# Modulation weights between the units of a projection pair, the tokens' norm ahead of the memory's projections, GpSimd for the first low parts, gates behind the picks' rows

## The chip, the cores and the metric

The kernel runs on one core of a Trainium2 chip. The metric is the device time of one execution, in microseconds (us). TensorE multiplies matrices, VectorE (DVE in rows) and ScalarE (ACT) do elementwise work, GpSimd (POOL) does elementwise work and issues gathers, and SyncE (SP) issues the loads from HBM (the device's main memory).

## The reference

All is float32; there are 256 tokens of width 1024. Three parts follow each other, cut here to what matters:

```python
# block 1: one layer
h = rms_norm(x, g_mix); proj = h @ w_in            # 1024 -> 4352: three attentions' q, k, v
y_sb, y_dil, y_mem = stick_breaking(...), dilated(...), memory_attention(m_q, rms_norm(mem, g_mem))
gates = sigmoid(h @ w_gate + b_gate)
x = x + (gates[:,:,0]*y_sb + gates[:,:,1]*y_dil + gates[:,:,2]*y_mem) @ w_out
# product-key experts ("peer"): 8 heads, 16 picks of 16384 each
h2 = rms_norm(x, g_ffn); q = (h2 @ w_q).reshape(T, 8, 2, 128)
s1, i1 = top_k(sc[:, :, 0], 16); s2, i2 = top_k(sc[:, :, 1], 16)   # two lists of 128 scores
cand = s1[..., :, None] + s2[..., None, :]; top_s, pos = top_k(cand, 16)
idx = take_along(i1 * 128 + i2, pos); gate = softmax(top_s)
x = x + sum_k gate_k * gelu(u[idx_k] . h2) * v[idx_k]
# two diffusion-style layers: an mLSTM and a retention mixer, each followed by 16 experts (MoE);
# six modulation vectors per layer come from a condition vector: silu(c) @ ada_w + ada_b
```

The modulation vectors depend on the condition alone. Their weights (`ada_w`) can be loaded and multiplied at any time before the mixers.

## The kernel before, in words

Weights stream from HBM in slabs of 1 MB (128 partitions by 2048 floats) through a ring of slots, four of them in block 1. SyncE issues every load in the order in which the program asks for the slabs, and a load waits until its slot is free. A weight slab is two *units*. Each unit is split into a rounded high part on ScalarE (L608) and a low part, source minus high, on VectorE or GpSimd (L615); a list, `units.lo`, says which of the two engines makes the next low part (`None` is VectorE). The parts go to tiles named `rw_68` to `rw_71`, so at most four units are split at a time, at most two of them ahead of the unit in use. Three matrix products per tile (`mm3`, all at L627) then make up for a product in float32. The activations' two parts lie in `rt` tiles.

*Block 1* (`block1`): the memory's norm, its projection to keys and values in two pairs of slabs (`wide`, two slabs or four units, 48 matmuls of 512 columns), then the tokens' projections (`proj_task`), into which the three attentions are woven as side tasks. Twelve of the projections are pairs (`pair` 6 times, the gates 6 times). The modulation vectors are a task of their own, `ada_task`: one step of it takes one `ada_w` slab out of the ring and multiplies it (8 matmuls of 32 rows by 256 columns, 16 records in the trace), and a projection says how many steps follow it. A modulation slab is not split; its slot is free when its 8 matmuls are done.

*Peer* (`prepare`, `route`, `picks`): `prepare` makes scores in eight slabs of queries; after slabs 0, 1, 3 and 7 it runs `route` for the heads at hand, which finds the 16 best picks of each head on VectorE: top-16 of two lists (MAX8, FIND_INDEX8, MATCH_REPLACE8), of their sums, the softmax over the 16 (`gate`), and the row numbers (`rows`), whose last operation is the cast at L1481. `picks` then gathers, for each pick, a row of 8 KB for each of 128 tokens (256 gathers by GpSimd, L1352), multiplies it with the tokens on VectorE, and needs `gate` only after a Gelu over a batch of picks. The rest of `prepare` and the mLSTM's context are woven into the gathers.

The two mixers and the two MoE layers follow (`block2`); the MoE layers only stream weights and multiply them. A scheduler sets the final order on each engine from the program's order and its dependencies, so that an edit can also move instructions far from it.

Of the kernel before, what the change touches and what calls it, by code (L numbers as in the profile page):

```python
# [14 lines left out]
AF = mybir.ActivationFunctionType  # L15
OP = mybir.AluOpType
AX = mybir.AxisListType
# [492 lines left out]
class K:  # L510
# [264 lines left out]
                         (w[u][0].a[:, s], w[u][1].a[:, s]), c == 0, c == nk - 1)  # L775
        return p

    def wide(self, Ts, units):


        ps = [[self.ps() for _ in range(2)] for _ in Ts]
        for k, unit in enumerate(units):
            w = self.units.get(*unit)
            for T, p in zip(Ts, ps):
                for i in range(2):
                    for cc in range(2):
                        c = 2 * k + cc
                        h, f = slice(c * 256 + i * 128, c * 256 + i * 128 + 128), slice(cc * 512, (cc + 1) * 512)
                        self.mm3(p[i].a, (T[0].a[:, h], T[1].a[:, h]), (w[0].a[:, f], w[1].a[:, f]), c == 0, c == 2 * len(units) - 1)
            for b in w:  # L790
                b.free()
        return ps

    def halves(self, kind, s, *x):
# [51 lines left out]
    def block1(self, mem):  # L846
        mT = self.norm_T([m.a for m in mem], self.col("g_mem"), w=1024)
        for m in mem:
            m.free()
        self.ada_open()  # L850
        self.ada = self.ada_task([(0, k) for k in range(6)] + [(1, 0), (1, 1)])
        self.mkv = self.f(2048)

        mkv = self.mkv.v("p (i f) -> p i f", i=2)
        for s in range(2):
            for i, p in enumerate(self.wide([mT], self.halves("w1", 2 * s))[0]):
                self.act(mkv[:, i, s * 512:(s + 1) * 512], p.a)
                p.free()
            if s == 0:
                self.hT = self.norm_T([x.a for x in self.x], self.col("g_mix"))  # L860
        for b in mT:
            b.free()
        self.dil_buffers()
        self.drive(self.proj_task(), [self.mem_task(), self.sb_task(), self.dil_task()], 0.6)
        self.merge_task()
# [12 lines left out]
    def proj_task(self):  # L878
        nc = self.nc
        sbq = self.sbq.v("p (h t) -> p h t", h=8)  # L880
        nc.gpsimd.memset(self.sbq.a, 0.0)
        hT, W = self.hT, W1

        def pair(name, s, place):

            for i, p in enumerate(self.wide([hT], self.halves("w1", W[name] + 2 * s))[0]):
                for dst, a, b in place(i):
                    self.act(dst, p.a[:, a:b])
                p.free()
            self.ada_steps(2)  # L890

        def row(b, i, n, o=0):
            return b.a[:, i * n + o:i * n + o + 512]

        self.mq = self.f(2 * 512)
        pair("mq", 0, lambda i: [(row(self.mq, i, 512), 0, 512)])
        self.done.add("mq")
        yield 9800
        for s in range(4):
            w = self.wslab(("w1", W["sbqk"] + s))  # L900
            p = self.slab_T(hT, w)
            if s < 2:
                pv = p.v("p (b t) -> p b t", b=2)
                o = sbq[:, 4 * s:4 * s + 4].rearrange("p (b e) t -> p b e t", e=2)
                self.act(o[:64, :, 0], pv[:64])
                self.act(o[64:, :, 1], pv[64:])
            else:
                self.act(self.sbk.a[:, (s - 2) * 512:(s - 1) * 512], p.a)
            p.free()
            self.wfree(w)  # L910
            self.ada_steps(1)
            yield 5200
        pair("sbv", 0, lambda i: [(row(self.sbv, i, 512), 0, 512)])
        self.done.add("sbv")
        yield 9800
        for s in range(4):

            parts = []
            while len(self.dqkv) < (512 * s + 511) // 768 + 1:
                self.dqkv.append(self.f(2 * 768))  # L920
            for x in range(3):
                a, b = max(512 * s, 768 * x), min(512 * (s + 1), 768 * (x + 1))
                if a < b:
                    parts.append((x, a, b))
            pair("d", s, lambda i: [(self.dqkv[x].a[:, i * 768 + a - 768 * x:i * 768 + b - 768 * x], a - 512 * s, b - 512 * s) for x, a, b in parts])
            yield 9800
        w = self.wslab(("w1", W["dlast"]))
        p = self.slab_row(hT, w)
        self.act(self.dqkv[2].v("p (i f) -> p i f", i=2)[:, :, 512:], p.v("p (i f) -> p i f", i=2))
        p.free()  # L930
        self.wfree(w)
        self.done.add("dlast")
        self.ada_steps(1)
        yield 5200
        for s in range(6):
            if s % 2 == 0:
                self.gates.append(self.f(2048))
            b = self.bcast_row(f"bg{s // 2}", s % 2 * 512, 512)
            for i, p in enumerate(self.wide([hT], self.halves("w1", W["gate"] + 2 * s))[0]):
                o = row(self.gates[-1], i, 1024, s % 2 * 512)  # L940
                self.tt(o, p.a, b.a, OP.add)
                p.free()
            b.free()
            self.ada_steps(2)
            yield 9800

    def sb_task(self):
# [348 lines left out]
    def prepare(self, h2T):  # L1296

        self.sc = [self.plain(self.RA) for _ in range(2)]
        sub = self.stream.get(("w1", W1["sub"]))
        for s in range(8):  # L1300
            w = self.wslab(("w1", W1["pq"] + s))
            p = self.slab_T(h2T, w)
            q = self.f(512)
            self.act(q.a, p.a)
            p.free()
            self.wfree(w)
            p = self.ps()
            for i in range(2):
                for f in range(2):
                    self.mm(p.a[:, i * 256 + f * 128:i * 256 + f * 128 + 128], q.a[:, f * 256 + i * 128:f * 256 + i * 128 + 128],  # L1310
                            sub.a[:, (2 * s + f) * 128:(2 * s + f + 1) * 128])
            for i in range(2):
                self.act(self.sc[i].a[:, s * 256:(s + 1) * 256], p.a[:, i * 256:(i + 1) * 256])
            p.free(), q.free()
            yield 5200
            if s == 7:
                for b in h2T:
                    b.free()
                sub.free()
                self.stream.shrink(2)  # L1320
                self.units.lo = deque([None])
            if s in (0, 1, 3, 7):
                yield from self.route(0, {0: 0, 1: 1, 3: 2, 7: 4}[s], s + 1)
# [68 lines left out]
    def route(self, i, h0, h1):  # L1392

        V, n = self.nc.vector, h1 - h0
# [25 lines left out]
        top, pos = self.f(16 * n), self.f(16 * n)  # L1420
        tv = top.v("p (h k) -> p h k", h=n)
# [12 lines left out]
        gate, k1, k2 = r["gate"].a[:, c16], self.f(16 * n), self.f(16 * n)  # L1434
        pf = self.f(16 * n)
        V.tensor_copy(pf.a, pos.a.bitcast(U32))

        gv = gate.rearrange("p (h k) -> p h k", h=n)
        z = self.f(16)
        self.tt(gv, tv, tv[:, :, :1].to_broadcast([128, n, 16]), OP.subtract)  # L1440
        self.act(gate, gate, AF.Exp)
        V.tensor_reduce(z.a[:, :n], gv, axis=AX.X, op=OP.add)
        V.reciprocal(z.a[:, 8:8 + n], z.a[:, :n])
        self.tt(gv, gv, z.a[:, 8:8 + n].rearrange("p (h u) -> p h u", u=1).to_broadcast([128, n, 16]), OP.mult)
        for b in (z, top, pos):
            b.free()

        N = 16 * n
        ge, d1 = self.f(15 * N), self.f(15 * n)
        dv = d1.v("p (h k) -> p h k", h=n)  # L1450
# [29 lines left out]
        self.stt(k1.a, k1.a, 128.0, k2.a, OP.mult, OP.add)  # L1480
        V.tensor_copy(r["rows"].a[:, c16].bitcast(U32), k1.a)  # L1481
        for b in (pf, lf, k1, k2):
            b.free()
        r["heads"] = h1
        yield 950 * n
# [970 lines left out]
```

## Time and profile before

| what | value |
| --- | --- |
| time before, median of 3 runs | 2660.3 us (2659.62 to 2661.32) |
| profiled execution, device time | 2665.6 us |
| its span, first to last instruction | 2663.8 us |
| mean granted TensorE clock | 0.954 |
| block 1's projections, merge and norm | 0 to 400 us |
| routes and gathers (the first at 418.47 us) | 400 to 1240 us |
| mLSTM / MoE / retention / MoE | 1240 to 1460 / 1910 / 2190 / 2664 us |

The span lies 1.8 us below the profiled execution's own time, and that execution was 5.3 us longer than the median. Stages are read off the busy engines and the loads; they overlap by some us. In the rows further down, a tile's buffer number is left out, "[4.39 <-DMA x]" is the engine's idle time just before the row and what ended it, and PEclk is the TensorE clock granted, as a share of full speed.

### The profile page before, as it was taken

Reading aid. Unit: us, or ns where it says so; the run is one execution under the profiler, and the core shown is the slowest. Engines: PE = TensorE matmul, PEld = TensorE weight load, DVE = VectorE, ACT = ScalarE, POOL = GpSimd, SP = SyncE. Lnnn points to the kernel's source line nnn. Section 1 sums busy time; section 2 is a strip of 40 time slices with the busy share of each in tenths; the row PEclk is TensorE's granted clock in tenths of the full one; section 3 lists DMA queues with packets and bytes.
Section 4 is the critical chain, followed back from the end, with each engine's and each line's share of the span. In section 5 each row is a group of like instructions: output and inputs, shape, how many; then the busy total and the mean of one; then the engine's idle time right before and its main releaser. Section 6 shows DMA issues by size and latency. Waiting matters only on the chain. (4 is left out here: it accounts for less than half of the span.)

```text
span 2663.8 us, 28650 instructions
## 1 busy us (share of the span) xinstructions
PE 2280.4 (86%) x10507; PEld 1297.9 (49%) x10507; DVE 1233.6 (46%) x2818; ACT 750.2 (28%) x1490; POOL 628.5 (24%) x523
## 2 busy tenths in 40 slices
PE   7999977688777897777877999999969989888876
PEld 5867666355422553223766344444458873222213
DVE  5455458888945775555875122211277461000001
ACT  5554433233511643112653000000142440000000
POOL 4323434343344343333430000000022420000000
PEclk9999988999889999999988999999989999999999
DMA  8467647887899889997456899999966389999998
GB/s 301 173 238 271 220 166 295 332 311 300 308 384 414 307 346 380 418 412 295 143 179 240 339 404 409 409 409 409 387 217 241 120 348 386 409 410 409 409 409 273
DMA packets 195788, 854.60 MB, mean 321 GB/s; under 512 B 14654, under 2 KB 39822, under 8 KB 149312
## 3 DMA queue, kind: packets, MB, share of 16 engines
q1 hardware_dynamic: 153376, 569.30, 55.9%
q0 software_dynamic: 42272, 283.47, 27.5%
q8 instruction: 83, 1.36, 0.2%
q14 instruction: 57, 0.47, 0.0%
HBM read 851.53 MB, written 1.18 MB: 320 GB/s over the span
## 5 line engine op out<-in xcount | busy, mean ns | idle before, releaser
L627 PE MATMUL pp<-fa 128*128 128x512 f32 (+8 forms) x4912 | 1289.6, 495 | 249.1 <-ACT fa L608 180.1
L627 PEld LDWEIGHTS pp<-fa 128*128 128x128 f32 (+2 forms) x4912 | 568.5, 161 | 878.0 <-issue 444.6
L624 DVE SCALAR_TENSOR_TENSOR fa<-fa 128x1024 f32<-128x1024 f32 (+5 forms) x561 | 408.6, 749 | 190.0 <-DMA fa<-in_puv,fa 181.6
L627 PE MATMUL pp<-rw,rt 128*128 128x512 f32 (+1 forms) x1896 | 462.4, 399 | 11.4 <-DVE rw L615 2.3
L627 PEld LDWEIGHTS pp<-rw,rt 128*128 128x128 f32 x1896 | 354.2, 191 | 98.1 <-issue 10.2
L1352 POOL DMA_INDIRECT fa<-in_puv,fa x256 | 285.0, 1113 | 443.6 <-PE pp L627 332.9
L608 ACT ACTIVATE fa<-fa 128x256 f32<-128x256 f32 (+9 forms) x473 | 188.9, 423 | 564.6 <-DVE fa L624 409.8
L615 DVE TENSOR_TENSOR fa<-pp,fa 128x512 f32<-128x512 f32 (+3 forms) x225 | 128.1, 579 | 453.6 <-PE pp L627 437.9
L608 ACT ACTIVATE fa<-pp 128x512 f32<-128x512 f32 (+4 forms) x169 | 93.3, 565 | 750.2 <-PE pp L627 608.8
L608 ACT ACTIVATE rw<-fa 128x1024 fp32r<-128x1024 f32 x208 | 216.1, 1054 | 256.7 <-PE pp L627 172.9
L615 POOL TENSOR_TENSOR rw<-fa,rw 128x1024 fp32r<-128x1024 f32 x81 | 205.9, 2543 | 311.4 <-ACT rw L608 302.7
L627 PE MATMUL pp<-rt,rw 128*128 128x256 f32 x1632 | 229.4, 301 | 26.6 <-ACT rw L608 8.5
L627 PE MATMUL pp<-rt,fa 128*64 128x512 f32 (+3 forms) x736 | 239.0, 574 | 14.8 <-DMA rt<-in_moe_up 7.7
L615 DVE TENSOR_TENSOR rw<-fa,rw 128x1024 fp32r<-128x1024 f32 x127 | 174.7, 1382 | 155.6 <-ACT rw L608 152.5
L627 PEld LDWEIGHTS pp<-rt,rw 128*128 128x128 f32 x1632 | 214.1, 203 | 40.2 <-ACT rw L608 9.3
L627 PE MATMUL pp<-rw,fa 128*64 128x512 f32 (+2 forms) x720 | 205.1, 582 | 16.5 <-DMA rw<-in_moe_down 6.6
L621 DVE TENSOR_SCALAR fa<-pp,fa 128x128 f32<-128x128 f32 (+1 forms) x80 | 36.3, 461 | 243.7 <-PE pp L627 172.6
L615 DVE TENSOR_TENSOR fa<-fa 128x2 f32<-128x2 f32 (+12 forms) x325 | 101.0, 322 | 75.8 <-ACT fa L608 51.5
L627 PEld LDWEIGHTS pp<-rt,fa 128*64 128x64 f32 (+1 forms) x736 | 65.7, 124 | 115.8 <-issue 78.3
L637 PE MATMUL pp<-ct,fa 128*128 128x128 f32 (+3 forms) x441 | 75.0, 309 | 53.2 <-ACT fa L608 22.1
L627 PEld LDWEIGHTS pp<-rw,fa 128*64 128x64 f32 (+1 forms) x720 | 57.7, 123 | 124.9 <-issue 82.2
L680 POOL DMA_DIRECT2D fa<-in_rows x9 | 5.1, 570 | 431.8 <-PE pp L627 414.4
(135 smaller groups left out, 1007.6 us busy)
## 6 DMA issues: line engine op xcount, KB each, us to landing
fa<-in_w SPq DMA_DIRECT2D x105, 1024.0 KB, 5.9
fa<-in_moe_gate SPq DMA_DIRECT2D x72, 1024.0 KB, 15.2
fa<-in_moe_down SPq DMA_DIRECT2D x68, 1024.0 KB, 17.6
fa<-in_moe_up SPq DMA_DIRECT2D x60, 1024.0 KB, 18.2
fa<-in_ada_w SPq DMA_DIRECT2D x48, 1024.0 KB, 5.4
rw<-in_moe_up SPq DMA_DIRECT2D x36, 1024.0 KB, 18.1
rt<-in_moe_down SPq DMA_DIRECT2D x31, 1024.0 KB, 16.7
rt<-in_moe_up SPq DMA_DIRECT2D x28, 1024.0 KB, 17.8
```

Of the source, the lines that this page charges most:

```text
L608: return self.nc.scalar.activation(out, in_, func, **kw)
L615: (eng or self.nc.vector).tensor_tensor(out, a, b, op=op)
L621: (eng or self.nc.vector).tensor_scalar(out, a, s1, s2, op0=op0, op1=op1, **kw)
L624: self.nc.vector.scalar_tensor_tensor(out, a, s, b, op0=op0, op1=op1, **kw)
L627: self.nc.tensor.matmul(ps, l, r, start=start, stop=stop, skip_group_check=True)
L637: self.nc.tensor.transpose(ps, x, self.c("ident")[:k, :k])
L680: self.nc.gpsimd.dma_start(b.a, bass.AP(tensor=r.tensor, offset=r.offset + o, ap=[[0, 128], [1, n]]))
L1352: self.nc.gpsimd.indirect_dma_start(b, None, self.t["puv"], bass.IndirectOffsetOnAxis(ap=rows.bitcast(U32)[:, j:j + 1], axis=0))
```

## The change

There are four edits. The modulation steps of a pair, two behind its last unit before, now stand one behind the second of the four units and one behind the last (`between`). The tokens' norm (`norm_T` of `x`) is called ahead of the memory's projections, and not behind the first of their two pairs. In `prepare`, all low parts of the first slabs go to GpSimd, and from slab 2 on VectorE and GpSimd take turns again, as they did from the start before. In `route`, the softmax stands behind the rows.

```diff
-    def wide(self, Ts, units):
+    def wide(self, Ts, units, between=None):
 ...
             for b in w:
                 b.free()
+            if between and k == 1:
+                between()
         return ps
 ...
         self.ada_open()
         self.ada = self.ada_task([(0, k) for k in range(6)] + [(1, 0), (1, 1)])
+        self.hT = self.norm_T([x.a for x in self.x], self.col("g_mix"))
 ...
-            if s == 0:
-                self.hT = self.norm_T([x.a for x in self.x], self.col("g_mix"))
 ...
-            for i, p in enumerate(self.wide([hT], self.halves("w1", W[name] + 2 * s))[0]):
+            for i, p in enumerate(self.wide([hT], self.halves("w1", W[name] + 2 * s), lambda: self.ada_steps(1))[0]):
 ...
-            self.ada_steps(2)
+            self.ada_steps(1)
 ...
-            for i, p in enumerate(self.wide([hT], self.halves("w1", W["gate"] + 2 * s))[0]):
+            for i, p in enumerate(self.wide([hT], self.halves("w1", W["gate"] + 2 * s), lambda: self.ada_steps(1))[0]):
 ...
-            self.ada_steps(2)
+            self.ada_steps(1)
 ...
         sub = self.stream.get(("w1", W1["sub"]))
+        self.units.lo = deque([self.nc.gpsimd])
         for s in range(8):
 ...
             yield 5200
+            if s == 1:
+                self.units.lo = deque([None, self.nc.gpsimd])
 ...
-        gv = gate.rearrange("p (h k) -> p h k", h=n)
-        z = self.f(16)
-        self.tt(gv, tv, tv[:, :, :1].to_broadcast([128, n, 16]), OP.subtract)
-        self.act(gate, gate, AF.Exp)
-        V.tensor_reduce(z.a[:, :n], gv, axis=AX.X, op=OP.add)
-        V.reciprocal(z.a[:, 8:8 + n], z.a[:, :n])
-        self.tt(gv, gv, z.a[:, 8:8 + n].rearrange("p (h u) -> p h u", u=1).to_broadcast([128, n, 16]), OP.mult)
-        for b in (z, top, pos):
-            b.free()
 ...   (the same ten lines, now here:)
         V.tensor_copy(r["rows"].a[:, c16].bitcast(U32), k1.a)
         for b in (pf, lf, k1, k2):
+            b.free()
```

What this does to the order on the engines shows at three places. The first is the tokens' first pair (`mq`). On TensorE before, its last unit (`rw_71` with the tokens' parts `rt_66` and `rt_67`) is followed by 32 matmuls of the modulation (`fa`, 32x256), four slabs of it, and then by the memory task's transposes (L637):

```order
L627 MATMUL pp<-rw_71,rt_66 128x512
L627 MATMUL pp<-rw_71,rt_67 128x512
L627 MATMUL pp<-rw_71,rt_66 128x512 x2
L627 MATMUL pp<-rw_71,rt_67 128x512
L627 MATMUL pp<-fa 32x256 x32
L637 MATMUL pp<-ct,fa 128x128 x16
L627 MATMUL pp<-rt_66,rw_68 128x256
```

In the changed kernel 8 of them stand between the pair's second unit (`rw_69`) and its third (`rw_70`):

```order
L627 MATMUL pp<-rw_69,rt_67 128x512
L627 MATMUL pp<-rw_69,rt_66 128x512 x2
L627 MATMUL pp<-rw_69,rt_67 128x512
L627 MATMUL pp<-fa 32x256 x8
L627 MATMUL pp<-rw_70,rt_66 128x512 x2
L627 MATMUL pp<-rw_70,rt_67 128x512
```

The other 24 stand where all 32 stood, behind the last unit:

```order
L627 MATMUL pp<-rw_71,rt_67 128x512
L627 MATMUL pp<-rw_71,rt_66 128x512 x2
L627 MATMUL pp<-rw_71,rt_67 128x512
L627 MATMUL pp<-fa 32x256 x24
L637 MATMUL pp<-ct,fa 128x128 x16
L627 MATMUL pp<-rt_66,rw_68 128x256
```

So one slab of the four is used two units earlier. On SyncE the loads of that pair and of the slabs behind it stood in this order before (`in_w` weight slabs, `in_ada_w` modulation slabs):

```order
L572 DMA fa<-in_w 128x2048 x2
L579 DMA fa<-in_ada_w 128x2x1024 x2
L572 DMA fa<-in_w 128x2048
L579 DMA fa<-in_ada_w 128x2x1024
L572 DMA fa<-in_w 128x2048
L579 DMA fa<-in_ada_w 128x2x1024
L572 DMA fa<-in_w 128x2048 x2
```

In the changed kernel they take turns:

```order
L572 DMA fa<-in_w 128x2048
L579 DMA fa<-in_ada_w 128x2x1024
L572 DMA fa<-in_w 128x2048
L579 DMA fa<-in_ada_w 128x2x1024
L572 DMA fa<-in_w 128x2048
L579 DMA fa<-in_ada_w 128x2x1024
L572 DMA fa<-in_w 128x2048
L579 DMA fa<-in_ada_w 128x2x1024
L572 DMA fa<-in_w 128x2048 x3
```

In both there are four weight and four modulation slabs among the first eight of these loads, and the fourth modulation slab is the eighth.

The second place is the first route on VectorE, around its softmax (reduce L1442, reciprocal L1443, multiplication with 16 columns) and the low part of `rw_68`. Before:

```order
L615 TENSOR_TENSOR fa<-fa 128x15
L615 TENSOR_TENSOR rw_68<-fa,rw_68 128x1024
L1442 TENSOR_REDUCE fa<-fa 128x1
L1443 RECIPROCAL fa<-fa 128x1
L615 TENSOR_TENSOR fa<-fa 128x16
L615 TENSOR_TENSOR fa<-fa,ct 128x240
L615 TENSOR_TENSOR rt_2442<-fa 128x240
L1461 TENSOR_REDUCE fa<-rt_2442 128x16
```

In the changed kernel the end of the same route, with the rows' cast at L1475, reads:

```order
L615 TENSOR_TENSOR rt_2442<-rt_2442,fa 128x256
L1473 TENSOR_REDUCE fa<-rt_2442 128x16
L624 SCALAR_TENSOR_TENSOR fa<-fa 128x16
L1475 CAST fa<-fa 128x16
L615 TENSOR_TENSOR rw_70<-fa,rw_70 128x1024
L1483 TENSOR_REDUCE fa<-fa 128x1
L1484 RECIPROCAL fa<-fa 128x1
L615 TENSOR_TENSOR fa<-fa 128x16
L1405 MAX fa<-rt_2442 128x8 x2
```

The softmax and one low part (`rw_70`) stand behind the cast, where the softmax and both low parts stood ahead of it; the MAX of the second route follows.

The third place is GpSimd ahead of the first gathers. The tile `in_rows` holds the norm's weights as rows, and `mods` is the modulation vectors' place in HBM. Before, two low parts stand between a write to `mods` and four reads of it:

```order
L680 DMA fa<-in_rows 128x1024
L1229 DMA mods<-fa 4x256
L615 TENSOR_TENSOR rw_69<-fa,rw_69 128x1024
L615 TENSOR_TENSOR rw_71<-fa,rw_71 128x1024
L1502 DMA fa<-mods 16x128 x4
L1229 DMA mods<-fa 4x256
L1502 DMA fa<-mods 16x128 x2
```

In the changed kernel there are four of them, and two more ahead of the next two reads:

```order
L680 DMA fa<-in_rows 128x1024
L1230 DMA mods<-fa 4x256
L615 TENSOR_TENSOR rw_68<-fa,rw_68 128x1024
L615 TENSOR_TENSOR rw_69<-fa,rw_69 128x1024
L615 TENSOR_TENSOR rw_70<-fa,rw_70 128x1024
L615 TENSOR_TENSOR rw_71<-fa,rw_71 128x1024
L1506 DMA fa<-mods 16x128 x4
L1230 DMA mods<-fa 4x256
L615 TENSOR_TENSOR rw_68<-fa,rw_68 128x1024
L615 TENSOR_TENSOR rw_69<-fa,rw_69 128x1024
L1506 DMA fa<-mods 16x128 x2
```

Over the whole kernel the rows of TensorE and SyncE are as many as before; VectorE has 2409 instructions after 2412, GpSimd 531 after 528, and ScalarE's order holds 84 table loads after 74.

## Rows read from the trace of the kernel before

**Rows 1.** Windows: busy us (x instructions) by engine, PEclk, DMA share, GB/s.

```profile
0.00:100.00 100.00, 82.28 (x532) 70.43 (x533) 48.17 (x112) 56.82 (x94) 35.56 (x21) 0.95 0.68 252
...
500.00:600.00 100.00, 75.42 (x274) 41.80 (x273) 86.09 (x319) 35.24 (x78) 40.28 (x38) 0.95 0.86 321
...
740.00:1240.00 500.00, 396.56 (x1049) 186.20 (x1048) 293.58 (x634) 146.25 (x403) 199.10 (x194) 0.96 0.95 383
```

**Rows 2.** Waits of TensorE, 0 to 345: total us, times, longest.

```profile
PE pp L637 <- ACT fa L608: 10.1, 1, 10.1
PE pp L627 <- DMA fa<-in_ada_w: 5.9, 2, 4.4
PE pp L637 <- DVE fa L615: 5.1, 3, 3.1
```

**Rows 3.** TensorE in order of time: start us, us, instructions.

```profile
43.76 5.15 PE L627 MATMUL pp<-rw,rt 128*128 128x512 f32 x22
48.84 2.80 PE L627 MATMUL pp<-fa 128*32 128x256 f32 x48
56.03 1.94 PE L627 MATMUL pp<-fa 128*32 128x256 f32 x16 [4.39 <-DMA fa<-in_ada_w]
61.08 3.83 PE L637 MATMUL pp<-ct,fa 128*128 128x128 f32 x16 [3.12 <-DVE fa L615]
```

**Rows 4.** The load queue (SyncE) in order of time.

```profile
49.97 0.37 SPq L579 DMA_DIRECT2D fa<-in_ada_w  x1
50.83 1.20 SPq L572 DMA_DIRECT2D fa<-in_w  x2
```

**Rows 5.** The same windows view around the stall.

```profile
50.00:56.00 6.00, 1.64 (x32) 0.72 (x24) 2.60 (x3) 3.61 (x5) 1.77 (x1) 0.97 1.00 382
56.00:66.00 10.00, 6.85 (x39) 5.23 (x40) 7.23 (x22) 1.33 (x3) 1.27 (x2) 0.51 0.88 351
```

**Rows 6.** DMA issues, the page: count, KB each, median us to landing.

```profile
fa<-in_ada_w SPq DMA_DIRECT2D x48, 1024.0 KB, 5.4
```

**Rows 7.** TensorE in order of time, ahead of the routes.

```profile
385.41 6.50 PE L627 MATMUL pp<-rt,rw 128*128 128x256 f32 x35 [5.34 <-DVE rt L624]
```

**Rows 8.** VectorE in order of time, the first route.

```profile
400.37 0.49 DVE L1401 MAX8 fa<-rt 128x8 f32<-128x128 f32 x2 [0.38 <-ACT rt L608]
...
407.36 1.22 DVE L615 TENSOR_TENSOR rw<-fa,rw 128x1024 fp32r<-128x1024 f32 x1
...
408.90 2.03 DVE L615 TENSOR_TENSOR fa<-fa 128x16 f32<-128x16 f32 x1
410.96 0.41 DVE L615 TENSOR_TENSOR fa<-fa,ct 128x240 f32<-128x240 f32 x1
...
418.02 0.17 DVE L1481 CAST fa<-fa 128x16 uint32<-128x16 f32 x1
421.41 0.49 DVE L1401 MAX8 fa<-rt 128x8 f32<-128x128 f32 x2 [3.22 <-ACT rt L608]
```

**Rows 9.** GpSimd in order of time, the first route.

```profile
408.50 2.40 POOL L615 TENSOR_TENSOR rw<-fa,rw 128x1024 fp32r<-128x1024 f32 x1 [4.44 <-ACT rw L608]
...
418.47 1.04 POOL L1352 DMA_INDIRECT fa<-in_puv,fa  x1 [3.11 <-DVE fa L1481]
```

**Rows 10.** Groups of instructions: total us, mean ns, idle before.

```profile
L615 POOL TENSOR_TENSOR rw<-fa,rw 128x1024 fp32r<-128x1024 f32 x81 | 205.9, 2543 | 311.4 <-ACT rw L608 302.7 <-issue 7.8 <-DMA fa<-in_rows 0.7
...
L615 DVE TENSOR_TENSOR rw<-fa,rw 128x1024 fp32r<-128x1024 f32 x127 | 174.7, 1382 | 155.6 <-ACT rw L608 152.5 <-PE pp L627 2.7
...
L608 ACT ACT_TABLE_LOAD x74 | 94.9, 1283 | 16.7 <-DVE fa L619 5.7 <-issue 4.3 <-DVE fa L624 4.3
```

**Rows 11.** ScalarE in order of time.

```profile
418.23 0.60 ACT L608 ACTIVATE fa<-pp 128x512 f32<-128x512 f32 x1 [5.28 <-DVE fa L1481]
...
462.39 1.28 ACT L608 ACT_TABLE_LOAD   x1
463.68 0.23 ACT L608 ACTIVATE fa<-fa 128x32 f32<-128x32 f32 x1
```

More of the change, by code (lines that the diff above doesn't have):

```diff
@@ L1482, in route @@
         for b in (pf, lf, k1, k2):
+            b.free()
+        gv = gate.rearrange("p (h k) -> p h k", h=n)
+        z = self.f(16)
+        self.tt(gv, tv, tv[:, :, :1].to_broadcast([128, n, 16]), OP.subtract)
+        self.act(gate, gate, AF.Exp)
+        V.tensor_reduce(z.a[:, :n], gv, axis=AX.X, op=OP.add)
+        V.reciprocal(z.a[:, 8:8 + n], z.a[:, :n])
+        self.tt(gv, gv, z.a[:, 8:8 + n].rearrange("p (h u) -> p h u", u=1).to_broadcast([128, n, 16]), OP.mult)
+        for b in (z, top, pos):
             b.free()
```

## The prediction, as it was put on record

> **What bounds the kernel now.** The change touches block 1 and the peer part, so I read the stages first, by busy time in windows. TensorE fills 82 of the first 100 us; from 500 to 600 VectorE is busy 86 of 100 us and TensorE 75; from 740 to 1240 the DMA engines are busy 95% of the time [rows 1]. So the same microsecond is worth something on TensorE in block 1, on VectorE in the routes, and little while the gathers fill the DMA engines.
>
> Then the waits of TensorE in block 1 [rows 2]. It waits 10.1 us once, at the start, 5.9 us in two pieces for modulation slabs, and 5.1 us for VectorE in transposes. The 5.9 is the direct target of the first edit, and it is small: 0.2% of the kernel.
>
> Where it falls is seen on TensorE in order of time [rows 3]. Behind the last matmuls of the tokens' first pair, 48 modulation records run from 48.84 to 51.64, then TensorE stands 4.39 us until the fourth modulation slab is there, runs the last 16, and stands 3.12 us more for the memory task's chain on VectorE. The load queue shows why the slab is late [rows 4]: it is issued only at 49.97, 1.1 us after the first modulation matmuls began, so I take its slot to be one that they emptied; right behind it, at 50.83, two weight slabs are issued and share the engines with it. The windows show both the price of a slab and the aftermath [rows 5]: from 50 to 56 the DMA engines are full at 382 GB/s, by which 1 MB takes 2.7 us alone, and from 56 to 66 the granted clock is 0.51, which is the lower of its two levels (1.2 GHz of 2.4), behind an idle stretch of 7.5 us in two pieces. Ten us at 0.51 are 4.9 us of TensorE time lost.
>
> Last I read the first route on VectorE [rows 8], since nothing is gathered before its cast. From MAX8 at 400.37 to the cast at 418.02 it takes 17.65 us; the first gather is issued at 418.47 [rows 9].
>
> **The change part by part.** The sum is made against the profiled execution's 2665.6 us, and then moved to the median.
>
> *Modulation between the units.* No work is added: 8 matmuls and one load per step, as before, on the same queue. At the first pair, one slab of four is used two units earlier. A unit pair is 24 matmuls; 22 take 5.15 us [rows 3], so 24 take 5.6, and its slot comes free that much earlier. But the fourth modulation slab is the eighth load in both orders, and three of the four slabs are still used behind the pair. If its slot is the second modulation slab's, it is still issued near 50, and what improves is only what it shares the engines with: the weight slabs ahead of it have been issued earlier. If it gets a slot 5.6 us sooner, it lands before it is asked for. So this wait shrinks by 0 to 4.39 us; the median slab lands 5.4 us after its issue [rows 6], this one after 6.1 (56.03 less 49.97), so with no sharing I expect some 4, that is 2 us less wait. I take -2.0. The rest of the 5.9 us, 1.5 us at a later pair, goes or stays: -0.7. The 3.12 us behind it is a chain of the memory task, on ScalarE and VectorE; it began before, and the slabs that land earlier bring ScalarE's splits of weights out of its way. Bounds 0 and -3.1, taken -1.0. The clock: if the idle stretch shrinks from 7.5 to some 4.5 us, the fall may or may not come; bounds 0 and -4.9, taken -2.0. At the other eleven pairs TensorE hardly waits for modulation slabs, and there the edit costs and gives nothing, as long as the weight slabs behind them are early (see the rivals). Block 1: **-5.7**, between 0 and -13.
>
> *Norm ahead.* The same 16 transposes and the same operations on ScalarE and VectorE, earlier by one pair of slabs. TensorE waits at the start 10.1 us for the memory's own norm [rows 2], and the pair that follows hides the tokens' norm. If the cover fails, what waits is one unit, some 2.8 us (half of 5.6). Taken 0.
>
> *Low parts on GpSimd.* Three low parts of 1.2 us each [rows 8] leave VectorE: -3.7 at most. VectorE is not what ends the wait at all three; one that is seen to be is ahead of TensorE's 5.34 us wait at 385.41 [rows 7]. I take -1.2. Against it: GpSimd's mean for the operation is 2.5 us, VectorE's 1.4 [rows 10], and a low part that takes longer also delays its unit by 1.2 us; and the lock. From 408.50 to 410.90 GpSimd makes a low part, and a VectorE multiplication of 16 columns, lasts from 408.90 to 410.93 [rows 8, 9]: it held until GpSimd was done. Three moved parts could each hold VectorE by 2.0 us: 0 to +6.1, taken +1.0, since in the norm ahead of the routes VectorE itself waits for others.
>
> The Trainium skill states this lock as a rule (SBUF — State Buffer, Who interferes with whom): a VectorE operation with two SBUF inputs and a GpSimd operation that reads SBUF exclude each other, and the second to start is blocked until the first ends. The trace agrees with it in the row above, 2.03 us. By the rule alone the edit would be a loss wherever VectorE has such an operation in hand, 3 x (2.4 - 1.2) = +3.6 in place of -0.2.
>
> *Gates behind the rows.* Reduce, reciprocal and multiplication stand between 408.6 and 410.96 before, 2.4 us with the hold; they and one low part (1.2 us) go behind the cast, and four small operations of the modulation's columns (some 0.2 us each) come in. The first gather is then asked for about 3 us earlier. But VectorE stands 3.22 us ahead of the second route anyway [rows 8], because ScalarE's evacuation at 418.23 waits for the cast [rows 11]; that evacuation now waits for the softmax's end, whose buffers it takes over. So most of the 3 us is paid back one route later. Bounds 0 and -3, taken -0.8, with queued behind the late evacuation the score matmuls and the second route's MAX8.
>
> *Ten more table loads* on ScalarE, as the new order alternates functions more often. One takes 1283 ns [rows 10]: 12.8 us. ScalarE is busy 35 of 100 us there [rows 1], which hides most; where an Exp falls between a batch's Gelus it lies on a gather's way to its release. Bounds 0 and +12.8, taken +1.5.
>
> The Trainium skill (ScalarE: Activation LUTs, What ACT_TABLE_LOAD costs) puts a switch at 2.66 us, a drain of 1.38 us included. By that the ten would be 26.6 us. The trace does not show the drain: a load at 462.39 takes 1.28 us and the next activation starts at 463.68, 0.01 us behind it [rows 11].
>
> *The rest.* The scheduler reorders the context, the mLSTM and the retention too. I found no wait there that an edit addresses; 0, with about 5 us either way, the size of the one stall that this order has in block 1.
>
> Sum: -5.7 + 0 - 1.2 + 1.0 - 0.8 + 1.5 = **-5.2**, so 2660.4 for the profiled execution. That execution was 5.3 us above the median of the runs shown; against the median of 2660.3 the forecast is **2655 us**. The later stages only stream weights, so what is saved earlier I carry to the end in full.
>
> **The rivals.**
>
> *No gain.* The fourth slab is still the eighth load, its slot is still emptied behind the pair, and the wait stays; what the routes gain at the first gather the late evacuation takes back. For it: three of four slabs are used where they were. Against it: the sharing at 50.83. Time: 2657 to 2664.
>
> *Slower: the pair's second weight slab.* It now comes behind a modulation slab in the queue, 2.7 us later if the queue is what limits. Its split, 1.2 us on VectorE alone [rows 8], follows before the third unit can start. There are twelve pairs. For it: the ring has four slots, and in the new order a weight slab always waits for a modulation slab's slot. Against it: the DMA engines are busy 0.68 of block 1's first 100 us [rows 1], so loads have room. It decides from four pairs on: 4 x 2.7 = +11 against -5.2, that is 2666; at all twelve it would be 2687.
>
> *Slower by the lock.* This is the rule of the SBUF page above. As a mechanism here: four low parts in a row on GpSimd (9.6 us at 2.4) ahead of the four reads of `mods`, whose columns VectorE now copies in the middle of the first route. If VectorE stands there for the last of them, the first gather is later by up to 9.6 less 4.8 (two such parts stood there before), and with three holds of 2.0: +11 on -5.2, so 2666. It decides when the first gather is later than before, measured from the score's MAX8: over 18.1 us (418.47 less 400.37).
>
> *A larger gain.* The whole 7.5 us and the 4.9 us of clock return, and the first gather's 3 us are kept: -15, 2645.
>
> **How the numbers follow.** I give the forecast (2650 to 2657) 0.46, no gain 0.20, slower 0.18 (pair's slab 0.08, lock 0.10), the larger gain 0.16. A measurement of this kernel can tell about 0.2%, 5.3 us: faster below 2655.0, slower above 2665.6. Of the forecast's 0.46 some 0.30 lies below; with the larger gain that is 0.46 faster. The other 0.16 and 0.18 of no gain are 0.34 the same. Slower: 0.18 and 0.02 of no gain. The range 2644 to 2668 leaves out half of the larger gain's far end (0.08) and the slower cases' upper part (0.11).
>
> **What would show it.** In the changed profile: TensorE's wait for modulation slabs in block 1 below 4 us (before 5.9), and the clock's window behind it above 0.51; VectorE's chain from MAX8 to cast near 14.5 us, with the second route's MAX8 still some 20 us behind the first's; the span's saving complete before 740 us. I am wrong if weight slabs end TensorE's waits between a pair's units, if VectorE holds at GpSimd's low parts in the norm, or if the time moves behind 740 us, where I priced nothing.

## The result, and the profile after

The changed kernel takes 2678.9 us (median of 15 runs) where the kernel before takes 2660.6 us (15 runs of each): a ratio of 1.0063, with a 95% interval from 1.0048 to 1.0077. It is slower by 0.6%, about 17 us, where I forecast 5 us less; the time lies outside the range. Single executions of one and the same kernel spread over some 20 us (before: 2655.6 to 2673.3), so a trace alone places a difference only where it is large or repeats.

The profiled execution took 2680.3 us, close to its median. The windows that answer to [rows 1] look like a small gain and a small loss:

```profile
0.00:100.00 100.00, 79.55 (x495) 67.07 (x495) 45.01 (x110) 55.40 (x92) 32.32 (x21) 0.91 0.66 244
500.00:600.00 100.00, 77.46 (x244) 39.90 (x243) 90.24 (x353) 28.91 (x71) 42.97 (x39) 0.91 0.89 346
740.00:1240.00 500.00, 392.02 (x1044) 182.99 (x1043) 289.43 (x628) 150.30 (x404) 200.16 (x198) 0.97 0.96 383
```

TensorE does less in the first 100 us (79.55 after 82.28), and at a clock of 0.91. Its waits in block 1, beside [rows 2], say why:

```profile
PE pp L637 <- ACT fa L608: 10.0, 1, 10.0
PE pp L637 <- DVE fa L615: 5.6, 1, 5.6
...
PE pp L627 <- DVE rt L624: 2.6, 1, 2.6
PE pp L627 <- DMA fa<-in_ada_w: 2.2, 1, 2.2
```

The wait for modulation slabs fell from 5.9 to 2.2 us, as forecast. But a wait of 2.6 us for VectorE is new. The waits in transposes, 5.1 us in three pieces before, are 5.6 us in one piece, all of it for the memory task's chain, which had 3.1 us before. In order of time, beside [rows 3]:

```profile
16.30 10.08 PE L627 MATMUL pp<-rw,rt 128*128 128x512 f32 x36 [2.63 <-DVE rt L624]
...
47.13 1.07 PE L627 MATMUL pp<-fa 128*32 128x256 f32 x16
48.13 5.78 PE L627 MATMUL pp<-rw,rt 128*128 128x512 f32 x24
53.84 1.93 PE L627 MATMUL pp<-fa 128*32 128x256 f32 x32
57.98 1.92 PE L627 MATMUL pp<-fa 128*32 128x256 f32 x16 [2.21 <-DMA fa<-in_ada_w]
65.51 3.82 PE L637 MATMUL pp<-ct,fa 128*128 128x128 f32 x16 [5.62 <-DVE fa L615]
```

The first 16 modulation records stand between the units (47.13), the last 16 wait 2.21 us and not 4.39. But the first projection matmul starts at 16.30 us, 2.63 us behind the transposes, and what the modulation gave, the memory task's chain takes: 5.62 us in place of 3.12. So this transposes' row stands at 65.51, where it stood at 61.08.

Where the 17 us are is seen from the times at which the same instruction starts in each trace: the ninth and the last weight slab (`in_w`), the first and the last gather, the addition of the retention's output (the first VectorE row `pp<-pp,fa` behind its last head), and the end. The kernel before has two traces, the one shown ahead of the prediction and a second one (run e8, 2662.3 us).

| kernel | 9th slab | gather 1 | gather 256 | last slab | addition | span |
| --- | --- | --- | --- | --- | --- | --- |
| before | 50.83 | 418.47 | 1237.81 | 2131.17 | 2167.61 | 2663.8 |
| before, second trace | 50.81 | 417.02 | 1234.36 | 2126.39 | 2162.84 | 2660.6 |
| changed | 54.97 | 418.13 | 1237.61 | 2133.73 | 2183.81 | 2678.3 |

Up to the last gather the change is level with before: block 1 loses 4 us and the first route gives them back. From the last weight slab to the addition the kernel before needs 36.4 us, the changed one 50.1. That is 13.6 of the 14.4 us between the two spans, at a place that no edit touches. The rows there, first VectorE and then GpSimd, of the changed kernel:

```profile
2183.81 2.49 DVE L615 TENSOR_TENSOR pp<-pp,fa 128x512 f32<-128x512 f32 x4 [9.75 <-DMA fa<-mods]
```

```profile
2152.63 0.54 POOL L1506 DMA_DIRECT2D fa<-mods  x1 [5.03 <-PE pp L627]
2153.52 0.57 POOL L1957 DMA_DIRECT2D fa<-in_router  x1 [0.36 <-PE pp L627]
2163.18 2.41 POOL L615 TENSOR_TENSOR rw<-fa,rw 128x1024 fp32r<-128x1024 f32 x1 [9.09 <-ACT rw L608]
2173.32 2.42 POOL L615 TENSOR_TENSOR rw<-fa,rw 128x1024 fp32r<-128x1024 f32 x1 [7.74 <-ACT rw L608]
2175.68 0.56 POOL L1495 DMA_DIRECT2D fa<-mods  x1
```

and of the kernel before:

```profile
2167.61 0.70 DVE L615 TENSOR_TENSOR pp<-pp,fa 128x512 f32<-128x512 f32 x1 [3.40 <-PE pp L627]
```

```profile
2116.21 0.53 POOL L1502 DMA_DIRECT2D fa<-mods  x1 [0.29 <-POOL fa L615]
...
2155.93 0.59 POOL L1491 DMA_DIRECT2D fa<-mods  x1 [10.81 <-PE pp L627]
2160.13 2.39 POOL L615 TENSOR_TENSOR rw<-fa,rw 128x1024 fp32r<-128x1024 f32 x1 [3.62 <-ACT rw L608]
2169.65 2.40 POOL L615 TENSOR_TENSOR rw<-fa,rw 128x1024 fp32r<-128x1024 f32 x1 [7.13 <-ACT rw L608]
```

The retention's output is multiplied with a row of modulation, broadcast to all partitions by a load on GpSimd's queue (L1491, L1495 after; 512 KB). Before, it is issued at 2155.93, ahead of two low parts. After, it is issued at 2175.68, behind them, and VectorE waits 9.75 us for it. The cause is seen one row earlier: the modulation's columns, which feed the router, are read at 2152.63 and not at 2116.21, after a wait for TensorE. By the program's rule for handing out tiles the row takes the router's place in both kernels. What differs is what lay there last: before, a row of the retention's gate that was done with early; in the changed kernel, the decay matrix that the last head multiplies with. So the columns, the router and the row, which all lie there, come late together, and the row last.

### The profile page after: what moved, and what is told of

Its sections match the earlier page's. It is cut to its first block, busy times and chain, and to the rows that moved or that the text cites. A ratio compares the mean times of both kernels' runs of the same rounds, so it can differ in the third digit from the quotient of the medians.

```text
span 2678.3 us, 28688 instructions
## 1 busy us (share of the span) xinstructions
PE 2279.8 (85%) x10507; PEld 1294.3 (48%) x10507; DVE 1237.3 (46%) x2815; ACT 763.7 (29%) x1500; POOL 628.8 (23%) x526
## 4 chain that ended last, share of the span: by engine, by line
PE 33%; DMA 23%; DVE 8%; issue 6%; ACT 3%; POOL 3%; SPq 1%; POOLq 0%; DVEq 0%; ACTq 0%
PE pp L627 32%; DMA fa<-in_puv,fa 7%; DVE fa L624 3%; DMA fa<-in_moe_down 3%; DMA rw<-in_moe_down 2%; POOL fa L1356 2%; ACT fa L608 2%; DMA rt<-in_moe_up 1%; DMA fa<-in_moe_up 1%; DMA rw<-in_moe_up 1%; DMA rw<-in_moe_gate 1%; DMA fa<-in_moe_gate 1%; DVE fa L615 1%; ACT L608 1%; DMA fa<-in_ada_w 1%
## 5 line engine op out<-in xcount | busy, mean ns | idle before, releaser
L627 PE MATMUL pp<-fa 128*128 128x512 f32 (+9 forms) x4912 | 1284.0, 493 | 242.7 <-ACT fa L608 167.9
L608 ACT ACTIVATE fa<-fa 128x128 f32<-128x128 f32 (+10 forms) x473 | 188.3, 423 | 567.9 <-DVE fa L624 411.0
L615 POOL TENSOR_TENSOR rw<-fa,rw 128x1024 fp32r<-128x1024 f32 x84 | 212.0, 2526 | 351.4 <-ACT rw L608 334.1
L637 PE MATMUL pp<-ct,fa 128*128 128x128 f32 (+3 forms) x441 | 77.3, 315 | 59.7 <-ACT fa L608 25.0
L608 ACT ACT_TABLE_LOAD x84 | 107.8, 1283 | 20.4 <-DVE fa L619 6.3
```

The source lines that it names most:

```text
L608: return self.nc.scalar.activation(out, in_, func, **kw)
L615: (eng or self.nc.vector).tensor_tensor(out, a, b, op=op)
L627: self.nc.tensor.matmul(ps, l, r, start=start, stop=stop, skip_group_check=True)
L637: self.nc.tensor.transpose(ps, x, self.c("ident")[:k, :k])
```

## The experiments

Each run is beside the kernel before on the same chip; ratios carry 95% intervals.

**The row called first (e1), and the gates alone (e2).** e1 is the changed kernel with one line moved, so that the row gets a tile of its own:

```diff
+        m2 = self.mod(1, 0, 2)
         self.mod_cols(1, [(0, 1)])
         self.M = self.moe_open(1, 1)
-        m2 = self.mod(1, 0, 2)
```

> The changed kernel, with one line moved: the broadcast of the modulation row that the retention's output is scaled with is called ahead of the router's opening and so gets a tile of its own. Theory A (the loss is that row's broadcast, held until the router's tile is free and queued behind two low parts on GpSimd): the end is no longer 14 us late, about 2664 us, 13 to 17 us below the changed kernel, and TensorE's 6.2 us wait near 2187 is gone. Theory B (the loss comes from the edits' own places, table loads and locks among them): no more than 3 us below the changed kernel, about 2677.

2668.5 us, 1.0036 [1.0020, 1.0052] of before: by the ratios 7 us less than the changed kernel, by the medians, which come from two chips, 10. That is more than theory B gave and less than theory A. The wait for the row is gone:

```profile
2156.79 0.59 POOL L1495 DMA_DIRECT2D fa<-mods  x1 [10.41 <-DVE fa L624]
2164.84 2.41 POOL L615 TENSOR_TENSOR rw<-fa,rw 128x1024 fp32r<-128x1024 f32 x1 [7.47 <-ACT rw L608]
```

```profile
2172.33 0.70 DVE L615 TENSOR_TENSOR pp<-pp,fa 128x512 f32<-128x512 f32 x1 [3.38 <-PE pp L627]
```

So the row is some 7 to 10 us of the loss of 17, not all of it: about 10 us are left. e2 has the softmax behind the rows and nothing else.

> The kernel before with the gates behind the rows alone. Theory A (this edit shifts the tiles' places, and so the late broadcast comes with it): 10 to 15 us slower than before, 2671 to 2676, and all of it behind 2130 us. Theory B (the edit costs or gives only in the routes): within 3 us of before, and any difference is there by the last gather.

2671.9 us, 1.0052 [1.0034, 1.0071]. The gates alone bring the wait, `[9.48 <-DMA fa<-mods]` at 2170.71 in its trace, and a loss of the size that theory A gave. In the routes they cost nothing: its first gather is issued at 414.03 and its last at 1224.41, ahead of both traces of before.

**All but the gates (e3), block 1 alone (e4).** Their diffs are the change's own, without the gates' edit, and the first two edits only.

> The change without the gates' edit. Theory A: the broadcast stands ahead of the low parts as before, so no loss at the retention's end: 2655 to 2664, within 5 us of before. Theory B: most of the 18 us stays, 2672 or more. My prediction's sum without its gates term (-0.8) would be 2656.

> The kernel before with the two edits of block 1 alone (modulation between the units, the tokens' norm ahead). My prediction's terms: -5.7 us, 2655, and the first gather some 5.7 us earlier. The changed kernel's trace against it: slabs are issued 4 to 6 us later in block 1, so the first gather is 3 to 6 us later. The end: 2660 to 2666 if that is carried through, and no late broadcast in either case.

2666.8 us, 1.0028 [1.0010, 1.0045], and 2668.0 us, 1.0029 [1.0014, 1.0044]. Neither has the late row. Both are some 8 us above before, more than I expected of either, with the ninth slab at 54.9 in both. The low parts on GpSimd, the one edit between the two, change nothing that can be measured. What is left of the loss comes with the edits of block 1.

**Which edit of block 1 (e5, e6, e11).**

> The kernel before with the modulation between the units alone. If this edit makes block 1 shorter (the wait for the fourth slab was 2.0 us in the run with both block 1 edits, 4.4 before), slabs behind the first pair are issued 2 to 5 us earlier and the time is 0 to 6 us below before. If it is the one that costs block 1 its 4 to 5 us, they are issued that much later and the time is 3 to 9 us above before.

> The kernel before with the tokens' norm ahead of the memory's projections alone. If VectorE and ScalarE serve the tokens' norm while TensorE waits for the memory's (the 2.6 us wait at 16.2 us in the run with both block 1 edits), the first projection matmul starts near 16.2 in place of 13.4 us and the ninth weight slab is issued 3 to 5 us later; the time is 3 to 9 us above before. If the norm costs nothing, both stay within 1 us and the time within 3.

Modulation between the units alone: 2660.6 us, 1.0003 [0.9987, 1.0019], no change. The norm ahead alone: 2678.6 us, 1.0072 [1.0051, 1.0094]. Its trace is of its fastest execution, 2666.9 us, so there is a second run of it:

> The tokens' norm ahead alone, once more, since its profiled execution lay 12 us under its own median: a second trace and a second time. If the 19 us are its own, 2672 to 2682 again; if they were that chip's, 2662 to 2668, as block 1's 4 us and the run with both block 1 edits (9 us above before) would have it.

2678.3 us, 1.0059 [1.0042, 1.0076]: the loss is its own. Alone it costs more than with the modulation's edit beside it (e4).

**The norm in other banks (e12).** In the program's order the first projection of the memory now takes the next two PSUM banks behind the tokens' norm. The banks are handed out in turn, eight in all, four to each norm's transposes: so these two are the first two that the memory's own transposes used, and the matmul must wait until those are read. e12 sets two banks aside for the projection; by the same rule it and the tokens' norm then get the banks that they have in the kernel before:

```diff
+        held = [self.ps(), self.ps()]
         self.hT = self.norm_T([x.a for x in self.x], self.col("g_mix"))
+        self.B.idle.extendleft((held[1].i, held[0].i))
```

> The tokens' norm ahead alone, but with the two PSUM banks set aside that the memory's first projection would have had, so that it no longer takes the banks of the memory's own transposes; no operation is added or left out. If the norm's edit costs at the start by that bank, the first projection matmul starts at 13.2 to 13.5 us again (16.2 to 16.5 with the norm alone) and the ninth weight slab is issued within 1 us of before. If all of the edit's 17 us follow from it, 2658 to 2664; if the start's 4 us are all that it explains, 2670 to 2675.

2662.2 us, 1.0004 [0.9992, 1.0015]: the whole loss is gone. TensorE at the start, in the run with the norm alone (e11) and in e12:

```profile
10.21 3.68 PE L637 MATMUL pp<-ct,fa 128*128 128x128 f32 x16 [10.21 <-ACT fa L608]
16.51 9.94 PE L627 MATMUL pp<-rw,rt 128*128 128x512 f32 x36 [2.62 <-DVE rt L624]
```

```profile
9.93 3.67 PE L637 MATMUL pp<-ct,fa 128*128 128x128 f32 x16 [9.93 <-ACT fa L608]
13.25 12.68 PE L627 MATMUL pp<-rw,rt 128*128 128x512 f32 x50
```

The 2.62 us wait is absent, the ninth slab is issued at 50.96 (55.41 in e11), the first gather at 419.81 (427.30). How 4 us at the start become 17 at the end these runs don't show in one place: in e11 the distance to the second trace of before is 4.6 us at the ninth slab, 10.3 at the first gather, 19.8 at the last gather; in e6, the same kernel, 4.4, 3.1 and 4.2.

**The gates, repaired (e7), and the frees alone (e9).** e7 is e2 with the row called first.

> The gates behind the rows, and the modulation row's broadcast called ahead of the router's opening. If the late broadcast is all that the gates' edit costs, 9 to 13 us below the run with the gates alone, 2659 to 2663, level with before or below it by as much as the first gather's 4 us. If the gates' edit costs in the routes as well, 2664 or more.

2661.0 us, 1.0008 [0.9993, 1.0023]: 11 us less than e2, level with before. In e9 no operation is moved in the program. Three tiles are given back later, and the scheduler's order follows from that:

```diff
-        for b in (z, top, pos):
-            b.free()
 ...
         for b in (pf, lf, k1, k2):
             b.free()
+        for b in (z, top, pos):
+            b.free()
```

> The kernel before with no operation moved in the program: only the three tiles of the softmax (z, top, pos) are given back behind the rows, as in the changed kernel, and not ahead of them. If the gates' edit costs by where tiles come to lie (the last head's buffer then lies where the router's tile and the broadcast row go), this kernel loses the same 10 to 14 us, 2669 to 2674, with VectorE waiting some 9.5 us for the modulation row near 2170. If it costs by the softmax's new place, this kernel is level with before, 2657 to 2662.

2666.7 us, 1.0034 [1.0018, 1.0049]; the wait is there:

```profile
2159.28 2.40 POOL L615 TENSOR_TENSOR rw<-fa,rw 128x1024 fp32r<-128x1024 f32 x1 [7.90 <-ACT rw L608]
2161.63 0.55 POOL L1491 DMA_DIRECT2D fa<-mods  x1
```

```profile
2169.16 2.49 DVE L615 TENSOR_TENSOR pp<-pp,fa 128x512 f32<-128x512 f32 x4 [9.14 <-DMA fa<-mods]
```

So it is the place of the tiles, not the place of the softmax, that makes the row late: buffers are cut from the smallest hole that fits, and three frees in another order lead to other holes some 1700 us later. The loss is smaller than I expected (5 to 9 us against 10 to 14).

The frees also do in the first route what my prediction put down to the softmax's place. In e9 the softmax still stands ahead of the cast (its multiplication at 410.89), and yet MAX8 to cast takes 14.32 us, the first gather following at 414.10:

```profile
399.33 0.49 DVE L1401 MAX8 fa<-rt 128x8 f32<-128x128 f32 x2 [0.38 <-ACT rt L608]
...
407.81 2.61 DVE L615 TENSOR_TENSOR rt<-fa 128x240 f32<-128x240 f32 x1
...
410.89 0.17 DVE L615 TENSOR_TENSOR fa<-fa 128x16 f32<-128x16 f32 x1
...
413.65 0.17 DVE L1479 CAST fa<-fa 128x16 uint32<-128x16 f32 x1
413.78 1.23 DVE L615 TENSOR_TENSOR rw<-fa,rw 128x1024 fp32r<-128x1024 f32 x1
```

One low part now stands behind the cast, and between 407 and 414 one operation is stretched beside a low part of GpSimd (2.61 us), where before has two, the 2.03 us of [rows 8] and this one:

```profile
413.25 2.14 DVE L615 TENSOR_TENSOR fa<-fa 128x16 f32<-128x16 f32 x1
```

By the last gather e2, e7 and e9 are at 1221.39 to 1224.41, 10 to 16 us ahead of both traces of before. Behind it they lose that again: from the last gather to the addition e2 and e9 need 946 and 948 us, e7 937, before 930 and 928. The row is some 9 of these 16 to 19 us; where the others go these runs don't show.

**Without the norm, row first (e10), and all with both repairs (e13).**

> The change without the norm's edit, and with the modulation row's broadcast called first: modulation between the units, low parts on GpSimd, gates behind the rows. If the norm's edit and the late broadcast are all that costs in the change, level with before or a little below, 2654 to 2662. If the low parts on GpSimd cost (lock, longer splits), 2663 to 2668.

2654.0 us, 0.9976 [0.9964, 0.9988]: faster than both kernels. Its first gather is issued at 408.42 and its last at 1220.62. The edits measured singly (e5, e7) are level with before, so the gain of some 6 us is not their sum, and no run shows which of them gives it.

> The whole change with both repairs: the broadcast row called first, the first projection in its own banks. If the two repairs take away all that the change costs, 2651 to 2658, like the run without the norm's edit. If the norm ahead costs beyond the start, 2660 to 2666 (2668.5 with the row first alone, less 4).

2678.1 us, 1.0074 [1.0055, 1.0092]: a miss. Block 1 is repaired (ninth slab 50.92, first gather 413.02, last 1234.10), the row is not waited for, and yet 53.6 us pass from the last weight slab (2120.42) to the addition (2173.99), where before needs 36.4. TensorE stands there at other places:

```profile
2132.97 1.22 PE L627 MATMUL pp<-fa 128*128 128x128 f32 x4 [2.54 <-DVE fa L624]
...
2168.34 1.43 PE L637 MATMUL pp<-ct,fa 128*128 128x128 f32 x4 [3.12 <-DVE fa L624]
```

The order of the last heads and of the output's products differs again. The same stretch took 45 us in e12, which lost nothing by its median, though its traced execution was 10 us above it (2672.3). What sets this stretch in e13 I have not settled.

**Before once more (e8).**

> The kernel before once more, for a second trace: its profiled execution lay 5 us above the median. If the gathers are what varies from run to run, block 1 and the two MoE layers repeat within 1 us, and the last gather does not.

2662.3 us. The ninth slab is issued at the same time within 0.02 us; by the last gather the two traces differ by 3.4, by the last slab by 4.8 us. So they drift apart all along, in the gathers and in MoE and retention too, and not in the gathers alone.

## Why the prediction was wrong, step by step

**The step that failed is "The rest ... I found no wait there that an edit addresses; 0, with about 5 us either way".** No edit addresses one, but the gates' edit makes one: the broadcast row behind two low parts, 7 to 10 us by e1 against the changed kernel, 11 by e7 against e2. It could have been read beforehand: the order of the changed kernel has the row's load behind the two last low parts on GpSimd, and before it stands ahead of them. My argument looked at the order only where the edits are. Bounding the rest by the size of a stall in block 1 was the wrong neighbour: at the retention's end the load queue issues nothing from 2177 to 2200 us before and from 2183 to 2213 in the changed kernel, so a late addition there goes with late loads for the next MoE.

**"Norm ahead ... Taken 0" failed too.** I had put its failing cover at 2.8 us; the wait at the start measured 2.6, and 4.1 by the ninth slab. That the sizes lie so close is luck, for the cause is none that I named: not the tokens' norm in the way on VectorE but the banks that it takes. And the time was not bounded by it: 16 and 19 us alone (e11, e6), none with other banks (e12), 14 to 16 between e1 and e10, which differ by this edit. In the whole change the banks are not all of it: e13 has them repaired and is as slow as the changed kernel.

**Modulation between the units, -5.7.** The mechanism was right: the last modulation records waited 2.21 us in the changed kernel, 1.53 in e5 and 0.52 in e10, after 4.39; I had said some 2 us less. The two terms behind it were mis-sized. The memory task's chain did not get shorter (-1.0 taken): in e10 TensorE waits 6.04 us for it in place of 3.12, so 1.4 us remain of the gain (transposes at 59.65, before 61.08). The clock did not come back (-2.0 taken): in the changed kernel it is 0.60 from 56 to 66 and 0.71 from 66 to 76; before it is 0.51 (0.59 in the second trace) and then 1.00. Alone the edit is worth nothing that can be measured (e5).

**Low parts on GpSimd, -1.2 + 1.0.** As small as taken (e3 beside e4), and the lock is there. VectorE's two operations of 1024 columns with the row of weights took 6.17 us while GpSimd made four low parts in a row; before they took 3.45 beside the end of one:

```profile
382.23 6.17 DVE L624 SCALAR_TENSOR_TENSOR fa<-fa 128x1024 f32<-128x1024 f32 x2 [3.04 <-DMA fa<-in_rows]
...
403.34 0.48 DVE L1405 MAX8 fa<-rt 128x8 f32<-128x128 f32 x2
...
411.78 2.61 DVE L615 TENSOR_TENSOR rt<-fa 128x240 f32<-128x240 f32 x1
...
417.68 0.17 DVE L1475 CAST fa<-fa 128x16 uint32<-128x16 f32 x1
...
422.80 0.49 DVE L1405 MAX8 fa<-rt 128x8 f32<-128x128 f32 x2 [3.21 <-ACT rt L608]
```

```profile
377.07 10.25 POOL L615 TENSOR_TENSOR rw<-fa,rw 128x1024 fp32r<-128x1024 f32 x4 [3.13 <-ACT rw L608]
388.69 1.97 POOL L1506 DMA_DIRECT2D fa<-mods  x4 [1.37 <-DVE fa L624]
...
411.42 2.70 POOL L615 TENSOR_TENSOR rw<-fa,rw 128x1024 fp32r<-128x1024 f32 x1 [4.43 <-ACT rw L608]
418.13 1.88 POOL L1356 DMA_INDIRECT fa<-in_puv,fa  x1 [4.01 <-DVE fa L1475]
```

TensorE's wait behind them was 6.62 us at 389.63, after 5.34 [rows 7]: the low part that left VectorE gave nothing. The rule of the Trainium skill on VectorE and GpSimd (SBUF — State Buffer, Who interferes with whom) agrees with these rows: a product of 240 columns, 0.41 us alone by [rows 8], took 2.61 beside a low part of GpSimd. The rival by the lock, +11, did not come: three low parts leave VectorE, and the first gather was issued 14.8 us behind the score's MAX8, where 18.1 was the mark.

**Gates behind the rows, -0.8.** The numbers came out in the first route: from MAX8 (403.34) to the cast (417.68) 14.34 us, 14.5 forecast, 17.65 before; the second route's MAX8 19.46 us behind the first's, forecast some 20, with the same 3.21 us wait ahead of it. The mechanism did not: e9 has the same 14.3 us with the softmax where it was, so the place of the softmax gives nothing there that the three frees don't give, and that 14.5 was met is luck. e7 gives the edit no measurable worth by itself.

**Ten more table loads, +1.5.** 84 loads of 1283 ns each in the trace, as ordered. e9, whose program moves no operation, has 80: the number follows the scheduler's order. No run separates their price.

**The rivals.** "Slower: the pair's second weight slab" did not come: alone the edit is level with before. That the time would move behind 740 us stood in the text as what would make it wrong, without a price.

## What to carry to other kernels

Where a scheduler and allocators of tiles and banks stand between the program and the chip, an edit's price is not at the edit alone: look through the whole order for loads that changed sides with work on the same queue, and at who waits for them, before pricing anything. A tile or bank that is taken or given back at another place in the program is part of the change, even if no operation moves (e9, e12). And an edit that lost time should be tried again with the collision taken out before it is dropped: the same edits without the norm, with one row called first, are 0.24% faster than before. It need not work: the whole change with both collisions taken out (e13) is as slow as without.

## What the runs showed of the hardware

The lock between VectorE and GpSimd stretched a VectorE operation from 0.41 to 2.61 us, and a pair of large ones from 3.45 to 6.17. Executions of one program differ by some 20 us on one core (before, beside e1: 2651.5 to 2673.0 in 25 runs, at granted clocks of 0.951 to 0.959). With 11 runs beside 22 of before the interval of e9 is 0.31% wide, and a single trace can lie 12 us below its own median (e6).
